# S5 block scan as a one-level tree, and GpSimd's share of the stage on VectorE

## The chip, the cores and the metric

The kernel runs on one core of a Trainium2 chip. The metric is the device time of one execution in microseconds (us), lower is better. Five engines take part: TensorE (PE, with its weight loads PEld), VectorE (DVE), ScalarE (ACT), GpSimd (POOL) and SyncE (SP, which here only issues transfers). Each engine runs its own instructions in order. DVE, ACT, POOL, SP and PE wait for one another by semaphores.

## The reference, cut to what matters

One encoder block over 1024 positions of width 1024. After a norm, one projection gives the columns z, xBC and dt of a Mamba-2 head group, and u of an S5 head group. Only the S5 scan is touched by the change. It has 64 channel groups, each with 64 complex states, and runs in both directions:

```python
bu_re = einsum("blgh,gph->blgp", ug, bb_re)        # and bu_im
_, _, h_re, h_im = lax.associative_scan(_complex_linear_combine, (a_re, a_im, bu_re, bu_im), axis=1)
y = einsum("blgp,ghp->blgh", h_re, c_re) - einsum("blgp,ghp->blgh", h_im, c_im)
```

That is the recurrence h[t] = a h[t-1] + bu[t] with a constant complex a for each state. After it follow a gated linear unit, the output projection and a feed-forward part, none of which the change touches.

## The kernel before, in words

**The scan.** The 1024 positions are cut into 128 blocks of 8. A matmul per block yields the block's own sum of states; a recurrence over the 128 blocks, with a to the eighth power (rcA real, rcB imaginary), turns the sums into the states at the block ends. They lie in one tile `SH` of 128 partitions by [direction 2, block 128, component 2, group pair 32], f32. A step of the recurrence (`rec_step`, L621 to 631) takes both directions at once: four VectorE operations of 128 elements a partition, two products (L628, L629) and two sums (L630, L631). There are 127 steps.

**The batch stage** (about 96 to 216 us of the profile). `s_batch(b)`, b = 0 to 7, makes the block sums of 8 groups: VectorE builds powers times B (L542 to 544, 896 elements each), PE transposes them (L550), ACT copies (L551), PE multiplies with u (L558), ACT copies the result into `SH` (L561), one element every 256 bytes. The tile `bp` between VectorE and PE has one buffer. Between the batches stand projection blocks on PE (`u_block`, `xbc_block`). This part is ordered by the planner from priorities and its own cost model; `sA` and `sB` are priorities for weight splits, `sb` for batches.

**The block stage** (about 216 to 434 us), under `tc.manual_schedule()`: the order on each engine is the order of the program text. 18 blocks n = 0 to 17: nine of xBC, one of dt, eight of z. An xBC or z block is 48 matmuls of 512 columns: three for each of 8 row chunks and two halves, because each weight is split in two f32r parts, `whi` (an ACT cast, L267) and `wlo` (raw minus whi, L268, one operation of 1024 elements). `wlo` is POOL's for xBC and z (`pl` = XZ), VectorE's elsewhere. `ensure` issues the split of block n+1 at the head of block n. ACT copies the two halves out of PSUM (L595 for xBC, L604 for z). After a block's matmuls the text has `run_steps(8)`, then one piece of the convolution `convs()`: on even n up to 10 a scaling on ACT (L719) and four VectorE operations (L724); on odd n the ACT silu of that result (L735), its store by SP (L737) and the load of the next channel block. For n = 11 to 14 it also has `c_dir`, 3 operations of 512 elements for each of two directions (L673 to 675), on POOL for these four batches (`pcd`), and one block later the small products `k_mm` (L692) on PE. The steps end with n = 15.

**The y stage** (about 442 to 545 us), also in text order: `restack` copies `SH` into `AH` (L770, eight copies for each of 16 batches, seven of them ACT's), `y_mm` multiplies with a table W0 (L780) and with AH (L781, L782), ACT applies gelu (L789). Then follow the gated unit, the Mamba-2 units, the output projection and the feed-forward part, up to 1695 us.

Of the kernel before, what the change touches and what calls it, by code (L numbers as in the profile page):

```python
# [9 lines left out]
F32 = mybir.dt.float32  # L10
# [5 lines left out]
ADD, SUB, MUL = ALU.add, ALU.subtract, ALU.mult  # L16


def _ap(t, off, dims):

    return bass.AP(tensor=t.tensor, offset=t.offset + off, ap=[list(t.ap[0])] + [list(d) for d in dims])
# [3 lines left out]
KN = {'s0': -800,  # L25
 'sA': 8,
 'sB': 50,
 'sG': -8,
 'sF': 20,
 'rec': 0,  # L30
 'cb': 8,
 'kb': -100,
 'w0': 0,
# [39 lines left out]
 'mq': 's',  # L73
 'pd': ['ef00', 'm00', 'xw1', 'yz0'],
 'yo': 0,
 'gst': 0,
 'g4': 800,
 'g6': -8,
# [1 line left out]
 'h6': 800,  # L80
 'fs': 0,
 'mc': 0,
 'pl': 'XZ',
 'pcd': [0, 1, 2, 3, 4, 5, 6, 7],
 'cd': [0, 1, 2, 3],
 'cB': [9, 11, 0, 1, 2, 3],
 'xq': 0,
# [1 line left out]
 'pc': [],  # L89
 'pk': [0, 1, 3, 4],  # L90
 'KC': 7,
 'r1': 8,
 'r2': 0,
 'r3': 0,
 'gs': 'asssssss',
 'gt': 'sasasasa',
# [36 lines left out]
def hymba_block(ctx, tc, P, out, dbg=None, upto=99):  # L133
    nc = tc.nc

    @contextmanager
    def hpri(n):
        off = KN[n]
        if off:
            p = tc.cur_priority  # L140
            tc.cur_priority = p - off
        yield
        if off:
            tc.cur_priority = tc.cur_priority + off

    def pri(n):
        def deco(f):
            def g(*a, **k):
                with hpri(n):
                    return f(*a, **k)  # L150
            return g
        return deco

    act, dve, pool, pe, sp = nc.scalar, nc.vector, nc.gpsimd, nc.tensor, nc.sync
# [10 lines left out]
    def newstack():  # L165
        e = ExitStack()
        stacks.append(e)
        return e
# [29 lines left out]
    def pacc():  # L198
        return psA.tile([128, 512], F32, tag="acc", name="acc")

    def ptmp():
        return psB.tile([128, 512], F32, tag="tmp", name="ptmp")
# [91 lines left out]
    rcA = rep.tile([128, 2, 2, 32], F32, name="rcA")  # L294
    rcB = rep.tile([128, 2, 2, 32], F32, name="rcB")
# [221 lines left out]
    @pri("lu")  # L517
    def load_u(b):
        U = sa.tile([128, 8, 128], F32, tag="U", name="U")
        sp.dma_start(U, u_d[8 * b:8 * b + 8].rearrange("g s h k -> (s h) g k"))  # L520
        return U

    def pw4(t, d, n0, nn, g0, ng):

        v = t[:, n0 - 1:n0 - 1 + nn, 64 * d + g0:64 * d + g0 + ng].rearrange("p n g -> p g n")
        return v.unsqueeze(3).to_broadcast([128, ng, nn, 16])

    def spread(t, nn):
        return t.unsqueeze(2).to_broadcast([t.shape[0], t.shape[1], nn, 16])

    @pri("sb")
    def s_batch(b, U):
        g0 = 8 * b
        yt = sa.tile([128, 2, 2, 8, 16], F32, tag="yt", name="yt")
        for y in range(2):
            sp.dma_start(yt[:, y].rearrange("p d g h -> p d (g h)"), y12_d[y][:, :, 16 * g0:16 * g0 + 128])
        bp = sa.tile([128, 2, 8, 8, 16], F32, tag="bp", name="bp")
        tm = sa.tile([128, 8, 7, 16], F32, tag="tmb", name="tmb")
        act.copy(_ap(bp, 0, [[1024 + 16 * 7, 2], [128, 8], [1, 16]]), yt[:, 0])
        for d in range(2):  # L540
            dst = _ap(bp, 16 if d == 0 else 1024 + 96, [[128, 8], [16 if d == 0 else -16, 7], [1, 16]])
            dve.tensor_tensor(dst, spread(yt[:, 0, d], 7), pw4(arR, d, 1, 7, g0, 8), op=MUL)  # L542
            dve.tensor_tensor(tm, spread(yt[:, 1, d], 7), pw4(aiR, d, 1, 7, g0, 8), op=MUL)
            dve.tensor_tensor(dst, dst, tm, op=ADD)
        for hb in range(2):
            bm = sa.tile([128, 2, 4, 128], F32, tag="bm", name="bm")
            for d in range(2):
                t = ptmp()
                for g in range(4):
                    pe.transpose(t[:, 128 * g:128 * g + 128], bp[:, d, 4 * hb + g].rearrange("p s h -> p (s h)"), ident)  # L550
                act.copy(bm[:, d].rearrange("p g c -> p (g c)"), t)  # L551
            for q in range(2):
                t = ptmp()
                for d in range(2):
                    for comp in range(2):
                        for j in range(2):
                            g = 2 * q + j
                            pe.matmul(t[64 * j:64 * j + 64, 256 * d + 128 * comp:256 * d + 128 * comp + 128],  # L558
                                      bm[:, d, g, 64 * comp:64 * comp + 64], U[:, 4 * hb + g, :], start=True, stop=True)
                pq = (g0 + 4 * hb + 2 * q) // 2  # L560
                act.copy(SH[:, :, :, :, pq].rearrange("p d k c -> p d c k"),  # L561
                         t.rearrange("p (d c k) -> p d c k", d=2, c=2))
# [6 lines left out]
    def u_half(b, hf):  # L569
        ps = pacc()  # L570
        gemm(b, hTh[hf], hTl[hf], HF[0], ps)
        u_evac(b, hf, ps)
# [10 lines left out]
    def u_block(b):  # L583
        ensure(b + 1)
        for hf in range(2):
            u_half(b, hf)

    def xbc_block(i):
        b = XORD[i]
        ensure(XBC0 + i + 1)  # L590
        xp = io.tile([128, 1024], F32, tag="io", name="xp")
        for hf in range(2):
            ps = pacc()
            gemm(XBC0 + i, hTh[hf], hTl[hf], HF[0], ps)
            act.copy(xp[:, HF[hf]], ps)  # L595
        aq.dma_start(xbc_d[128 * b:128 * b + 128, :], xp)
# [23 lines left out]
    @pri("rec")  # L620
    def rec_step(j):  # L621
        def at(k, swap=False):

            return _ap(SH, 64 * k + (32 if swap else 0),
                       [[8192 + 64 * (127 - 2 * k), 2], [-32 if swap else 32, 2], [1, 32]])
        m = rt.tile([128, 2, 2, 32], F32, tag="rm", name="rm", bufs=2)
        n = rt.tile([128, 2, 2, 32], F32, tag="rn", name="rn", bufs=2)
        dve.tensor_tensor(n, rcB, at(j - 1, True), op=MUL)  # L628
        dve.tensor_tensor(m, rcA, at(j - 1), op=MUL)  # L629
        dve.tensor_tensor(n, n, at(j), op=ADD)  # L630
        dve.tensor_tensor(at(j), m, n, op=ADD)  # L631

    steps = iter(range(1, 128))

    def run_steps(n):
        for _ in range(n):
            j = next(steps, None)
            if j is not None:
                rec_step(j)
# [39 lines left out]
    @pri("kb")  # L679
    def k_batch(b):  # L680
        k_mm(b)
        k_out(b)
# [49 lines left out]
    @pri("cs")  # L732
    def conv_silu(ct, xp, a, one=False, store=True):
        if one:
            act.activation(a, a, AF.Silu, scale=2.0)  # L735
            if store:
              sp.dma_start(xs_d[128 * ct:128 * ct + 128, :], a)  # L737
            return
        act.activation(xp, a, AF.Tanh)
        dve.scalar_tensor_tensor(a, xp, 1.0, a, op0=ADD, op1=MUL)  # L740
        if store:
            sp.dma_start(xs_d[128 * ct:128 * ct + 128, :], a)
# [500 lines left out]
    SH = shp.tile([128, 2, 128, 2, 32], F32, name="SH")  # L1243
    sst = newstack()
    sa = sst.enter_context(tc.tile_pool(name="sa", bufs=1, side="right"))
    for b in range(3, 8):
        s_batch(b - 3, load_u(b - 3))
        u_block(b)
    cv = None
    for b in range(5, 8):  # L1250
        s_batch(b, load_u(b))
        xbc_block(b - 5)
        if cv:
            conv_silu(*cv, one=True)
        if b > 5:
            cv = conv_taps(XORD[b - 6], sa)
    conv_silu(*cv, one=True)
    sst.close()
    ckst = newstack()
    ck = ckst.enter_context(tc.tile_pool(name="ck", bufs=1, side="right"))  # L1260
    rst = newstack()
    xt_load(0)
    rt = rst.enter_context(tc.tile_pool(name="rt", bufs=1, side="right"))
# [34 lines left out]

    cvs = convs()
    KC = KN["KC"]  # L1300
    with tc.manual_schedule():
        next(cvs)
        for n, blk in enumerate(blocks):
            blk()
            run_steps(KN["r1"])
            next(cvs, None)
            run_steps(KN["r2"])
            b = n - NB + KC
            if 0 <= b < 4:
                c_open(b)  # L1310
                c_dir(b, 0)
                run_steps(KN["r3"])
                c_dir(b, 1)
            if 0 < b < 4:
                k_batch(b - 1)
            if 0 <= b + 1 < 5 and n < NB - 1:
                xt_load(b + 1)
        run_steps(127)
        if KC == 4:
            xt_load(4)  # L1320
        next(cvs, None)
# [292 lines left out]
    def at(t, fn, *a):  # L1614
        tl.append((t, len(tl), fn, a))
# [104 lines left out]
    for l in range(8):  # L1720
        b = MX["step"] * l
# [11 lines left out]
        for q in range(2):  # L1733
            at(b + MX["ev"] + 0.6 * q, turn_evac, l, q)
            if l < 4 or q:
                n = "12"[q] + "12"[l // 4]
# [29 lines left out]
    for i in range(4, 14):  # L1766
        t = 2.56 * (i - 4)
# [13 lines left out]
    for i in range(14, len(prods)):  # L1781
        p, n, m = prods[i]
# [186 lines left out]
```

## Time and profile before

| | us |
|---|---|
| median of 3 runs | 1693.84 (1693.69 to 1709.21) |
| the profiled execution, its own time | 1697.36 |
| its span, first to last instruction | 1695.7 |
| PE busy | 1557.0 (92%) |
| VectorE busy | 1252.1 (74%) |
| ScalarE busy | 728.0 (43%) |
| GpSimd busy | 537.6 (32%) |

The busy shares are means over all stages. In the rows further down, a line names the code line, engine, operation, tile written and tiles read; "x" a count; a bracket at the end of a timeline row the idle time of the engine before it and what ended that. A row of busy time by stage has the stretch, its length, the busy us (and instructions) of PE, PEld, DVE, ACT and POOL, the granted clock as a share of full speed, the DMA share and GB/s.

### The profile page before, as it was taken

The numbers are of one execution on the slowest core, as the hardware profiler recorded it, in microseconds if no ns is written. First come the engines' busy times: TensorE is split into PE (matmuls) and PEld (weight loads), VectorE is DVE, ScalarE is ACT, GpSimd is POOL, SyncE is SP. The second block draws the span as 40 slices with busy tenths as digits, with TensorE's granted clock in tenths as the row PEclk, the third lists the DMA queues.
The fourth block names the chain that finished last, engine by engine and source line by source line (L and its number), as shares of the span: only waits on it lengthen the run. The fifth ranks groups of instructions, "written<-read, shape, count | busy, mean of one in ns | idle before, by whom it ended". The sixth has DMA issues, their size and how long they took to land.

```text
span 1695.7 us, 22363 instructions
## 1 busy us (share of the span) xinstructions
PE 1557.0 (92%) x7980; PEld 1270.2 (75%) x7980; DVE 1252.1 (74%) x2022; ACT 728.0 (43%) x1238; POOL 537.6 (32%) x499
## 2 busy tenths in 40 slices
PE   7998999889787879999998997999999999999897
PEld 6777788668675666778787775788888888787686
DVE  7445589999862567887576578788888788669777
ACT  6354632122598445444343277322222232344352
POOL 2111121157121020112111041555555555239512
PEclk9999999989799889999999998999999999999999
DMA  6543343243687748777668892333322221592234
GB/s 182 155 134 107 115 153 124 94 128 98 151 210 191 210 129 273 242 245 244 194 217 267 282 297 72 104 119 122 106 100 94 100 100 56 203 341 71 94 111 175
DMA packets 250003, 271.61 MB, mean 160 GB/s; under 512 B 29387, under 2 KB 190659, under 8 KB 249891
## 3 DMA queue, kind: packets, MB, share of 16 engines
q1 hardware_dynamic: 224515, 215.96, 41.2%
q0 software_dynamic: 12896, 33.83, 6.3%
q10 hardware_dynamic: 12480, 20.39, 3.4%
q8 instruction: 63, 1.03, 0.3%
q14 instruction: 49, 0.40, 0.1%
HBM read 185.23 MB, written 84.84 MB: 159 GB/s over the span
## 4 chain that ended last, share of the span: by engine, by line
PE 39%; DVE 10%; DMA 8%; issue 4%; ACT 3%; POOL 3%; SPq 0%; DVEq 0%; POOLq 0%; ACTq 0%
PE acc L1550 13%; PE ptmp L1550 10%; PE acc L1137 4%; PE ptmp L1856 4%; PE acc L1856 3%; DVE dop L1838 2%; DMA m<-m_d 2%; PE acc L277 1%; PE ptmp L956 1%; POOL wd L1823 1%; DMA m_d<-m 1%; DMA cl_d<-ghl 1%; DVE cacc L724 1%; PE ptmp L1022 1%; DMA graw<-g_d 1%
## 5 line engine op out<-in xcount | busy, mean ns | idle before, releaser
L277 PE MATMUL acc<-hTh,whi 128*128 128x512 f32 (+1 forms) x456 | 179.9, 395 | 8.5 <-ACT whi L267 8.0
L1137 PE MATMUL acc<-ohi,cat 128*128 128x512 f32 x512 | 175.7, 409 | 8.6 <-DMA cat<-ch_d 5.5
L277 PE MATMUL acc<-hTh,wlo 128*128 128x512 f32 (+1 forms) x456 | 179.1, 393 | 2.2 <-POOL wlo L268 2.1
L277 PE MATMUL acc<-hTl,whi 128*128 128x512 f32 (+1 forms) x456 | 179.4, 394 | 0.5 <-DVE hTl L337 0.5
L1533 DVE TENSOR_TENSOR wop<-rawp,wop 128x512 fp32r<-128x512 f32 x120 | 137.7, 1148 | 17.9 <-ACT wop L1532 16.7
L1550 PE MATMUL ptmp<-T,wop 128*128 128x512 f32 x528 | 127.9, 399 | 4.1 <-ACT T L1706 3.7
L1550 PE MATMUL acc<-T,wop 128*128 128x512 f32 x528 | 125.7, 393 | 1.6 <-DVE T L1709 1.5
L1856 PE MATMUL ptmp<-dop 128*128 128x512 f32 x528 | 122.2, 393 | 2.9 <-DVE dop L1838 2.9
L1550 PE MATMUL acc<-B,wop 128*128 128x512 f32 x528 | 124.6, 392 | 0.0
L1137 PEld LDWEIGHTS acc<-ohi,cat 128*128 128x128 f32 x512 | 99.3, 195 | 33.2 <-DVE s L1673 4.4
L1550 PEld LDWEIGHTS ptmp<-T,wop 128*128 128x128 f32 x528 | 101.2, 192 | 27.2 <-ACT T L1706 3.9
L268 POOL TENSOR_TENSOR wlo<-raw,whi 128x1024 fp32r<-128x1024 f32 x20 | 50.3, 2514 | 222.4 <-ACT whi L267 222.4
L1856 PEld LDWEIGHTS ptmp<-dop 128*128 128x128 f32 x528 | 100.2, 190 | 24.2 <-DVE dop L1838 3.2
L1550 PEld LDWEIGHTS acc<-T,wop 128*128 128x128 f32 x528 | 98.8, 188 | 24.9 <-DVE T L1709 3.3
L1550 PEld LDWEIGHTS acc<-B,wop 128*128 128x128 f32 x528 | 99.1, 188 | 21.7 <-DVE B L1709 0.2
L277 PEld LDWEIGHTS acc<-hTh,whi 128*128 128x128 f32 x456 | 87.1, 191 | 27.0 <-ACT whi L267 8.4
L1565 ACT ACTIVATE cg<-cg 128x512 f32<-128x512 f32 x44 | 27.8, 633 | 183.0 <-DVE cg L1563 182.9
L1838 DVE TENSOR_TENSOR dop<-da,dop 128x512 fp32r<-128x512 f32 x77 | 76.9, 999 | 36.7 <-ACT dop L1837 36.7
L1571 POOL TENSOR_TENSOR cg<-cg 128x512 f32<-128x512 f32 x44 | 61.8, 1405 | 130.5 <-DVE cg L1566 129.8
L277 PEld LDWEIGHTS acc<-hTh,wlo 128*128 128x128 f32 x456 | 87.1, 191 | 21.5 <-POOL wlo L268 4.1
L1532 ACT CAST wop<-rawp 128x512 fp32r<-128x512 f32 x120 | 70.2, 615 | 76.7 <-POOL rawp L1507 51.2
L1137 PE MATMUL acc<-olo,cat 128*128 128x512 f32 x256 | 103.1, 403 | 0.0
(362 smaller groups left out, 3566.1 us busy)
## 6 DMA issues: line engine op xcount, KB each, us to landing
ff_d<-cg POOLq DMA_DIRECT2D x77, 256.0 KB, 2.3
da<-ff_d SPq DMA_DIRECT2D x35, 512.0 KB
raw<-in_w_in_dram SPq DMA_DIRECT2D x28, 512.0 KB
cat<-ch_d SPq DMA_DIRECT2D x48, 256.0 KB
cat<-cl_d SPq DMA_DIRECT2D x48, 256.0 KB
wd<-in_w_down_dram SPq DMA_DIRECT2D x44, 256.0 KB
rawp<-in_w_gate_dram SPq DMA_DIRECT2D x10, 1024.0 KB
rawp<-in_w_up_dram SPq DMA_DIRECT2D x10, 1024.0 KB
```

The lines of the kernel that those rows point to most:

```text
L268: (pool if ("0" if j < 2 else "A" if j < XBC0 else "X" if j < Z0 else "Z" if j < GL0 else "G" if j < FF0 else "F") in KN['pl'] else dve).t ...
L277: pe.matmul(ps, a[:, k, :], b[:, k, sl], start=(k == 0 and n == 0), stop=(k == 7 and n == 2))
L724: (pool if ct in KN['pc'] and k in KN['pk'] else dve).scalar_tensor_tensor(a[:, d], xp[:, r], w[k], a[:, d], op0=MUL, op1=ADD)
L956: pe.matmul(t[:, 256 * s + 128 * d:256 * s + 128 * d + 128], Bt[:, c, g, :], Xw[:, d, c].rearrange("p h e -> p (h e)"), start=True, stop=True)
L1137: pe.matmul(ps, c[:, a, k % 4, :], b[:, k % 2, :], start=(k == 0 and n == 0), stop=(k == n_ - 1 and n == 2))
L1532: act.copy(t[:, 0], src)
L1533: dve.tensor_tensor(t[:, 1], src, t.bitcast(F32)[:, 0], op=SUB)
L1550: pe.matmul(ps, a[:, ai, k, :], b[:, bi, k, :], start=(k == 0 and q == 0), stop=(k == 3 and q == 2))
L1565: act.activation(cg[:, 0], cg[:, 0], AF.Silu)
L1571: pool.tensor_tensor(dst, a, b, op=op)
L1838: dve.tensor_tensor(t[:, k, 1], src, t.bitcast(F32)[:, k, 0], op=SUB)
L1856: pe.matmul(ps, t[:, 0, a, 128 * j:128 * j + 128], t[:, 1, b, :], start=(q == 0 and n == 0), stop=(q == NP - 1 and n == 2))
```

## The change

The scan becomes a tree of one level. (1) `pair_up(b)`, one for each of the 8 group batches and placed one batch behind `s_batch`, adds a times the first block's sum of each pair to the second's: 2 directions times 4 VectorE operations of 512 elements (64 pairs, 2 components, 4 group pairs). (2) `pair_powers` squares the power once: four operations of 128 elements. (3) `rec_step` runs over the 64 pair ends, 63 steps of the same four operations; 6 steps follow a block instead of 8, so that they end with n = 10. (4) `pair_down(d, c)` computes the 63 inner states of a direction from the pair ends: 8 calls of 4 operations of 1008 elements, one after each of the blocks 11 to 14, two after 15 and 16. (5) `pl` and `pcd` are emptied: 20 weight splits and 24 `c_dir` operations go from GpSimd to VectorE. The tile `up2` lies in the batch stage's pool `sa`, the tile `dn` shares the one buffer `cacc` with the convolution.

```diff
- 'pl': 'XZ',
- 'pcd': [0, 1, 2, 3, 4, 5, 6, 7],
+ 'pl': '',
+ 'pcd': [],
- 'r1': 8,
- 'r2': 0,
+ 'r1': 6,
...
-            return _ap(SH, 64 * k + (32 if swap else 0),
-                       [[8192 + 64 * (127 - 2 * k), 2], [-32 if swap else 32, 2], [1, 32]])
+            return _ap(SH, 64 * (2 * k + 1) + (32 if swap else 0),
+                       [[8192 + 64 * (125 - 4 * k), 2], [-32 if swap else 32, 2], [1, 32]])
...
-        dve.tensor_tensor(n, rcB, at(j - 1, True), op=MUL)
-        dve.tensor_tensor(m, rcA, at(j - 1), op=MUL)
+        dve.tensor_tensor(n, rcs[1], at(j - 1, True), op=MUL)
+        dve.tensor_tensor(m, rcs[0], at(j - 1), op=MUL)
...
-    steps = iter(range(1, 128))
+    steps = iter(range(1, 64))
+    rcs = []
+    def pair_powers():
...
+        dve.tensor_tensor(t, rcB, rcB, op=MUL)
+        dve.tensor_tensor(a2, rcA, rcA, op=MUL)
+        dve.tensor_tensor(a2, a2, t, op=SUB)
+        dve.scalar_tensor_tensor(b2, rcA, 2.0, rcB, op0=MUL, op1=MUL)
+    def advance(d, cur, prev, nk, q0, nq, t):
+        def at(k, swap=False):
+            return _ap(SH, 8192 * d + 64 * k + q0 + (32 if swap else 0), [[128, nk], [-32 if swap else 32, 2], [1, nq]])
+        for f, swap in ((rcA, False), (rcB, True)):
+            dve.tensor_tensor(t, f[:, d, :, q0:q0 + nq].unsqueeze(1).to_broadcast([128, nk, 2, nq]), at(prev, swap), op=MUL)
+            dve.tensor_tensor(at(cur), at(cur), t, op=ADD)
+    @pri("up")
+    def pair_up(b):
+        for d in range(2):
+            t = sa.tile([128, 64, 2, 4], F32, tag="up2", name="up2")
+            advance(d, 1 - d, d, 64, 4 * b, 4, t)
+    def pair_down(d, c):
+        t = ck.tile([128, 63, 2, 8], F32, tag="cacc", name="dn")
+        advance(d, 2 - d, 1 + d, 63, 8 * c, 8, t)
...
         s_batch(b - 3, load_u(b - 3))
+        if b > 3:
+            pair_up(b - 4)
         u_block(b)
...
         s_batch(b, load_u(b))
+        pair_up(b - 1)
         xbc_block(b - 5)
...
     conv_silu(*cv, one=True)
+    pair_up(7)
     sst.close()
...
         next(cvs)
+        pair_powers()
         for n, blk in enumerate(blocks):
             blk()
             run_steps(KN["r1"])
             next(cvs, None)
-            run_steps(KN["r2"])
+            if n == 10:
+                run_steps(64)
+            if n > 10:
+                for _ in range(1 if n < 15 else 2):
+                    if downs:
+                        pair_down(*downs.pop(0))
...
-        run_steps(127)
```

## Rows read from the trace of the kernel before

**Rows 1.** Busy time of each engine by stage: batch, block and y stage.
```profile
96.00:216.00 120.00, 113.06 (x898) 90.31 (x897) 69.00 (x68) 67.63 (x94) 15.70 (x13) 0.97 0.39 110
216.00:434.00 218.00, 203.19 (x934) 163.59 (x934) 204.51 (x492) 52.03 (x72) 76.91 (x59) 0.97 0.40 124
442.00:545.00 103.00, 79.32 (x718) 71.91 (x718) 53.27 (x88) 97.10 (x171) 21.83 (x40) 0.89 0.78 193
```

**Rows 2.** What PE waited for in the block stage.
```profile
PE acc L277 <- ACT whi L267: 8.0, 1, 8.0
PE ptmp L692 <- issue: 4.6, 1, 4.6
PE acc L277 <- POOL wlo L268: 2.1, 2, 1.3
```

**Rows 3.** ACT in order of time: copies of batch and block results, waits.
```profile
208.78 1.09 ACT L561 COPY SH<-ptmp 128x512 f32<-128x512 f32 x1
...
218.39 0.41 ACT L1267 CAST dtw<-dtr 128x256 fp32r<-128x256 f32 x1 [0.74 <-DMA xs_d<-cacc]
...
238.05 0.59 ACT L595 COPY xp<-acc 128x512 f32<-128x512 f32 x1 [4.85 <-PE acc L277]
...
248.93 0.59 ACT L595 COPY xp<-acc 128x512 f32<-128x512 f32 x1 [4.85 <-PE acc L277]
...
339.60 1.06 ACT L735 ACTIVATE cacc<-cacc 128x1024 f32<-128x1024 f32 x1 [15.51 <-DVE cacc L724]
...
441.51 4.57 ACT L770 COPY AH<-SH 64x254 f32<-64x254 f32 x7 [12.82 <-DVE SH L631]
```

**Rows 4.** PE in order of time, from the block stage into the y stage.
```profile
433.43 1.41 PE L692 MATMUL ptmp<-cp,yk 128*32 128x128 f32 x24
438.75 0.76 PE L780 MATMUL ptmp<-Uy,W 128*128 128x128 f32 x2 [3.92 <-issue]
```

**Rows 5.** VectorE in order of time: one undisturbed step, one disturbed product.
```profile
341.80 2.44 DVE L629 TENSOR_TENSOR rm<-rcA,SH 128x128 f32<-128x128 f32 x1
...
344.80 0.29 DVE L628 TENSOR_TENSOR rn<-rcB,SH 128x128 f32<-128x128 f32 x1
...
345.86 0.29 DVE L628 TENSOR_TENSOR rn<-rcB,SH 128x128 f32<-128x128 f32 x1
```

**Rows 6.** GpSimd in order of time, at the disturbed product.
```profile
341.67 2.42 POOL L268 TENSOR_TENSOR wlo<-raw,whi 128x1024 fp32r<-128x1024 f32 x1 [21.67 <-ACT whi L267]
```

**Rows 7.** VectorE's groups in the block stage, 216 to 443 us.
```profile
L629 DVE TENSOR_TENSOR rm<-rcA,SH 128x128 f32<-128x128 f32 x125 | 54.5, 436 | 0.0
L631 DVE TENSOR_TENSOR SH<-rm,rn 128x128 f32<-128x128 f32 x125 | 49.2, 393 | 4.3
...
L724 DVE SCALAR_TENSOR_TENSOR cacc<-xpad,vec,cacc 128x1022 f32<-128x1022 f32 x12 | 15.4, 1281 | 5.3 <-ACT cacc L719 5.1
```

**Rows 8.** GpSimd's groups in the block stage, 216 to 443 us.
```profile
L268 POOL TENSOR_TENSOR wlo<-raw,whi 128x1024 fp32r<-128x1024 f32 x16 | 39.2, 2450 | 138.0 <-ACT whi L267 137.9
L675 POOL TENSOR_TENSOR cp<-cp,tmc 128x512 f32<-128x512 f32 x8 | 11.4, 1429 | 0.6
...
L674 POOL TENSOR_TENSOR tmc<-xtc,aiR 128x512 f32<-128x512 f32 x8 | 9.1, 1142 | 0.0
```

**Rows 9.** VectorE over the whole span, shapes apart: split and c_dir there.
```profile
L268 DVE TENSOR_TENSOR wlo<-raw,whi 128x1024 fp32r<-128x1024 f32 x24 | 29.3, 1222 | 11.9 <-ACT whi L267 11.9
...
L673 DVE TENSOR_TENSOR cp<-xtc,arR 128x512 f32<-128x512 f32 x24 | 16.7, 695 | 15.5 <-DMA xtc<-x_d 15.2
```

**Rows 10.** VectorE's groups in the batch stage, 96 to 216 us.
```profile
L544 DVE TENSOR_TENSOR bp<-bp,tmb 128x896 f32<-128x896 f32 x16 | 21.7, 1355 | 0.2
...
L542 DVE TENSOR_TENSOR bp<-yt,arR 128x896 f32<-128x896 f32 x16 | 16.7, 1089 | 26.4 <-ACT bp L539 26.4
```

**Rows 11.** SP's queue in order of time: a convolution store.
```profile
215.58 0.33 SPq L737 DMA_DIRECT2D xs_d<-cacc  x1
```

More of the change, by code (lines that the diff above doesn't have):

```diff
@@ L75 @@
  'yo': 0,
+ 'up': 0,
  'gst': 0,
@@ L622, in at @@
         def at(k, swap=False):
-            return _ap(SH, 64 * k + (32 if swap else 0),
-                       [[8192 + 64 * (127 - 2 * k), 2], [-32 if swap else 32, 2], [1, 32]])
-        m = rt.tile([128, 2, 2, 32], F32, tag="rm", name="rm", bufs=2)
-        n = rt.tile([128, 2, 2, 32], F32, tag="rn", name="rn", bufs=2)
-        dve.tensor_tensor(n, rcB, at(j - 1, True), op=MUL)
-        dve.tensor_tensor(m, rcA, at(j - 1), op=MUL)
+            return _ap(SH, 64 * (2 * k + 1) + (32 if swap else 0),
+                       [[8192 + 64 * (125 - 4 * k), 2], [-32 if swap else 32, 2], [1, 32]])
+        m = rt.tile([128, 2, 2, 32], F32, tag="rm", name="rm")
+        n = rt.tile([128, 2, 2, 32], F32, tag="rn", name="rn")
+        dve.tensor_tensor(n, rcs[1], at(j - 1, True), op=MUL)
+        dve.tensor_tensor(m, rcs[0], at(j - 1), op=MUL)
         dve.tensor_tensor(n, n, at(j), op=ADD)
         dve.tensor_tensor(at(j), m, n, op=ADD)
-    steps = iter(range(1, 128))
+    steps = iter(range(1, 64))
+    rcs = []
+    def pair_powers():
+        t = rt.tile([128, 2, 2, 32], F32, tag="rm", name="rm")
+        a2 = rt.tile([128, 2, 2, 32], F32, name="rcA2")
+        b2 = rt.tile([128, 2, 2, 32], F32, name="rcB2")
+        dve.tensor_tensor(t, rcB, rcB, op=MUL)
+        dve.tensor_tensor(a2, rcA, rcA, op=MUL)
+        dve.tensor_tensor(a2, a2, t, op=SUB)
+        dve.scalar_tensor_tensor(b2, rcA, 2.0, rcB, op0=MUL, op1=MUL)
+        rcs.extend((a2, b2))
+    def advance(d, cur, prev, nk, q0, nq, t):
[12 more added lines that the diff above has]
+        advance(d, 2 - d, 1 + d, 63, 8 * c, 8, t)
     def run_steps(n):
@@ L1300, in hymba_block @@
     KC = KN["KC"]
+    downs = [(d, c) for c in range(4) for d in range(2)]
     with tc.manual_schedule():
         next(cvs)
+        pair_powers()
         for n, blk in enumerate(blocks):
```

## The prediction, made before the change was run

> **What bounds the kernel now.** I read busy time by stage first, then PE's waits, then the engine that the waits lead to. PE is busy 92% over all, so only a stage in which it stands still can give time. In the block stage [rows 1] PE lacks 14.8 us of 218, and VectorE is busy 204.5 of 218. PE's waits name others [rows 2]: 8.0 us for a weight cast on ACT, 4.6 at the small products, 2.1 for GpSimd's split. ACT is hardly loaded, so the cast was late for a reason: just ahead of it in ACT's order stands a silu that had waited 15.5 us for VectorE's convolution [rows 3]. The end of the stage is VectorE's too: the last matmul block ends at 433.4 [rows 4], but the restacking on ACT starts only at 441.5, released by the last step [rows 3]. Then ACT is busy 97 of 103 us [rows 1], so a y stage that begins earlier ends earlier by as much. In this stage VectorE sets the pace.
>
> Why is VectorE full? A step takes 1.06 us undisturbed, start to start [rows 5], and 127 make 135 us. But a product of 0.29 us lasted 2.44 while GpSimd ran a split of 2.42 us [rows 5, 6]. The steps' four groups (two of them stand in [rows 7]; the other two are like the second) hold about 54.5 + 3 x 49 = 201 us where 125 x 4 x 0.285 = 142 would do. So some 59 us of VectorE's busy time is waiting for GpSimd, whose splits and c_dir take 39.2 + 11.4 + 2 x 9.1 = 69 us there [rows 8]; the third c_dir group is like L674.
>
> **The change part by part.**
>
> *GpSimd's share.* 16 splits by 1.22 and 24 c_dir operations by 0.695 [rows 9] are 19.5 + 16.7 = 36 us on VectorE, against 59 us of waiting that goes: VectorE wins 23. GpSimd's order loses those operations; its small loads and stores come no later. A split is now behind VectorE's work of the block before; PE needs it about one block (10.88 us, [rows 3]) later.
>
> *Steps.* 64 fewer by 1.06 take 68 us off VectorE. The four operations of pair_powers cost 1.2.
>
> *Pair down.* 1008 elements: between 512 at 0.695 and 1024 at 1.222 [rows 9] a straight line gives 1.205, and with 0.03 between dependent operations 1.24. 8 x 4 x 1.24 = 40 us.
>
> *Pair up.* 512 elements at 0.695 + 0.03: 8 operations, 5.8 us for a batch, 46 us for eight. That is the batch stage's.
>
> The runs here are short: 8 adjacent elements below, 4 above; no row has VectorE on runs of 4. Low end: the 0.695 and 1.22 of [rows 9], since an operation of that size has not been seen cheaper. High end: ACT's copy into SH, with every element apart, took 1.09 against 0.59 for as many adjacent [rows 3], 1.85 times. I take the low end, because VectorE's own operations on runs of 16 [rows 10] say otherwise: 1.089 for 896 elements lies on the same line. [...]
>
> *The block stage, summed.* VectorE: steps 67, powers 1, down 40, splits 20, c_dir 17, convolution 24 x 1.28 = 31 [rows 7]: 176 us where it had 204. PE: its 203 busy us at a mean granted clock of 0.97 [rows 1] hide up to 203 x 0.03 = 6 us of low clock around its waits; I take 5. So PE could do the stage in 218 - 15 - 5 = 198 us. VectorE then has slack, and PE becomes the bound.
>
> *New waits.* (a) The last join starts when the last sums are in SH at 209.9 [rows 3] and after the four convolution operations that VectorE holds there, near 214.3; it ends near 220, the powers near 221.5. The block stage's tiles open only after it, where now they open when a store has landed, at 218.4 [rows 3]. The first split behind it is needed when block 0 ends, 238.05 - 10.88 = 227.2. Nothing is lost. (b) On even blocks the convolution waits for ACT's scaling after the block, so VectorE ends about 7 us behind PE; the next split comes 1.2 later, within 10.88. (c) The first pair_down shares its buffer with the last convolution: silu after block 11 (0.6 for the copy out, 1.06), then its store, which took from 215.58 to 218.39 [rows 3, 11], 2.8. So VectorE stands until 4.6 us after block 11, then needs 5.0 for pair_down and 6 x 0.695 = 4.2 for c_dir: 13.8. PE has finished block 12 at 10.88 and its k_mm stands for 2.9 us. Queued behind it is block 13. After that VectorE needs about 10.3 us a block and PE 10.88 plus k_mm: no more waits. VectorE is done some 6 us before the last block.
>
> PE's stage: 15 + 5 - 3 = 17 us sooner. *Handover.* PE's first product of the y stage waits for the table W0 until 5.3 us after the blocks [rows 4] and still will; but the restacking need no longer trail the blocks by 441.5 - 433.4 = 8.1, and can follow the last copy out at 0.6. ACT paces the stage, so 7.5 us more. What is late next there is W0, then ACT itself.
>
> *The batch stage.* VectorE idles 120 - 69 = 51 us [rows 1]. Seven joins (41) and four splits (5), less the waits for GpSimd in L544 (16 x (1.355 - 1.089) = 4, [rows 10]), make 42. The cover is VectorE's pause while PE and ACT work on a batch; a pause that is shorter than a join delays the next batch's products. I charge 3 us. Without cover the price is 46.
>
> Sum: -17 - 7.5 + 3 = -21.5. Against the profiled execution's 1697.36 that is 1675.9; it stood 3.5 above the median, and from 1693.84 I come to **1672 us**.
>
> **The rivals.**
>
> *Rival 1: joins stand in front of the next batch.* They come one batch behind, read SH while ACT writes its other columns, and their place in VectorE's order is the planner's. If half of each join (2.9 us) delays the next batch seven times, 20 us of the gain go: 1692. For it: little VectorE time is left over (42 of 51), and its products feed PE through one buffer. Against it: what delays L542 now is ACT [rows 10], a pause in which a join fits. Between this and the forecast every value from 1680 is possible.
>
> *Rival 2, the slower one: short runs cost as ACT's hopping does.* At 1.85 times, up is 85 us and down 73. The batch stage then needs 85 + 5 - 4 = 86 where 51 are idle: PE waits 35 us at the transposes. In the block stage VectorE has 209 us, more than PE's 198, so of the 24.5 only some 14 stay: 1693.84 + 35 - 14 = 1715. It decides once a join operation passes 51 / 56 = 0.9 us. For it: the ACT rows. Against it: VectorE's runs of 16 cost nothing extra.
>
> *Rival 3: the change frees VectorE but PE gains nothing,* because the cast waits for something else. Against it: the chain cast, silu, convolution is in the rows, and the 8.1 us at the end depend on no cast. Then only the 7.5 less the 3 would show: 1689. With rival 1 it lies within 1%.
>
> **How the numbers follow.** About 1% (17 us) is what a measurement of this kernel can tell from no change. Forecast 0.66: its own range is 1660 to 1682 (all of the batch stage's charge gone and 10 us more at the top, since low clock and waits may be undercounted; 10 us of lost charge below); 0.56 of it lies below 1677, 0.10 within 1%. Rivals 1 and 3 together 0.21, 1682 to 1694, of which 0.19 is within 1% and 0.02 faster. Rival 2 0.13: 0.12 slower, 0.01 within. Faster 0.58, same 0.30, slower 0.12. The range reaches over rivals 1 and 3 and leaves rival 2 and the edges out: 1660 to 1694.
>
> **What the profile after would show.** A step near 1.06 us everywhere in the block stage, no product of 2 us; 512-element joins near 0.7 and 1008-element ones near 1.2 (else rival 2); joins between L544 of one batch and L542 of the next, with PE's waits for L544 in the batch stage not above a few us (else rival 1); in the block stage no wait of 8 us for the cast, one of about 3 at k_mm; the blocks over near 416 to 419, the restacking right behind. I am wrong if PE's waits in the block stage stay at 15 us, if ACT still waits for VectorE at the restacking, or if the batch stage is over 10 us longer.

## The result, and the profile after

The changed kernel takes 1668.7 us (median of 4 runs, 1666.91 to 1674.15) against 1693.76 for the kernel before: 0.984 of it, 95% interval 0.981 to 0.987. That is 25 us by the medians, where the forecast was 22. The profiled execution took 1669.68 us, with a span of 1667.8.

Code lines from L634 on have moved by 32 to 43: the c_dir operations L673 to L675 are now L705 to L707, `k_mm` is L724 (was L692), the silu L767 (L735), the restacking L802 (L770), the W0 product L812 (L780), gelu L821 (L789). L652 is the product of a join, L653 its sum, both for `pair_up` and for `pair_down`.

Busy time by stage (as in [rows 1]); the last row is the y stage of this kernel, which begins 32 us sooner:

```profile
96.00:216.00 120.00, 116.56 (x928) 94.09 (x927) 105.95 (x125) 69.67 (x96) 4.70 (x9) 1.00 0.42 120
216.00:434.00 218.00, 207.83 (x1030) 170.36 (x1029) 177.31 (x372) 69.71 (x102) 13.49 (x27) 0.98 0.44 135
442.00:545.00 103.00, 77.62 (x606) 67.42 (x605) 47.41 (x81) 86.11 (x147) 20.23 (x34) 0.88 0.78 202
...
409.00:523.00 114.00, 88.17 (x773) 81.24 (x772) 54.32 (x86) 100.02 (x175) 24.84 (x47) 0.88 0.77 192
```

VectorE's work has moved from the block stage (204.5 to 177.3 us, and the stretch already holds the first 20 us of the y stage) into the batch stage (69.0 to 106.0), and PE is busier in both. PE's waits from 100 to 440 us, to be read beside [rows 2]:

```profile
PE ptmp L812 <- issue: 4.3, 1, 4.3
PE ptmp L558 <- ACT bm L551: 3.3, 6, 1.0
PE ptmp L724 <- issue: 3.3, 1, 3.3
PE ptmp L903 <- ACT AH L802: 2.6, 1, 2.6
```

The waits for a split or a cast are gone. What is left in the block stage is one at `k_mm`. VectorE's groups from 96 to 440 us, shapes apart:

```profile
L268 DVE TENSOR_TENSOR wlo<-raw,whi 128x1024 fp32r<-128x1024 f32 x22 | 26.8, 1219 | 1.7 <-ACT whi L267 1.7
L653 DVE TENSOR_TENSOR SH<-SH,up 128x512 f32<-128x512 f32 x32 | 22.0, 688 | 0.6
L653 DVE TENSOR_TENSOR SH<-SH,dn 128x1008 f32<-128x1008 f32 x16 | 19.3, 1208 | 0.6
L631 DVE TENSOR_TENSOR SH<-rm,rn 128x128 f32<-128x128 f32 x63 | 18.4, 292 | 2.2
...
L542 DVE TENSOR_TENSOR bp<-yt,arR 128x896 f32<-128x896 f32 x16 | 16.9, 1085 | 4.9 <-ACT bp L539 4.9
...
L652 DVE TENSOR_TENSOR dn<-rcA,SH 128x1008 f32<-128x1008 f32 x8 | 9.6, 1204 | 7.4 <-DMA xs_d<-cacc 7.4
```

The joins cost 688 and 1208 ns, the steps 292 where [rows 7] has 393 to 436, and before L542 VectorE now idles 4.9 us instead of 26.4 [rows 10]: that pause holds the joins. Four marks of each profile, in us, taken from the rows of ACT and PE in order of time, show where the time came from:

| | last copy of block 0 starts | last block matmul starts | last gelu is over | span |
|---|---|---|---|---|
| before | 227.17 | 433.11 | 546.25 | 1695.7 |
| after | 222.12 | 413.90 | 522.79 | 1667.8 |
| won since the mark before | 5.1 | 14.2 | 4.3 | 4.5 |
| after, run again beside later experiments | 227.62 | 418.27 | 528.83 | 1676.8 |
| won since the mark before | -0.5 | 15.3 | 2.6 | 1.5 |

The executions of before and after stood 3.5 and 1.0 us above their medians, the one run again 7.2. The 14 to 15 us at the blocks come in both executions of the changed kernel; the 5.1 ahead of them do not, so one execution tells the other stages to a few us only. What is won behind the last gelu belongs to the executions shown more than to the change: from there to the end it is 1149.5 us in the profile of before, 1145.0 in that of after, 1148.0 when it was run again, and 1143.9 to 1149.3 in the other ten experiments, one of them the kernel before with one edit ahead of this point (1146.9) and one with another (1146.4).

### The profile page after: what moved, and what is told of

It reads as the page before. It is cut to its first block, busy times and chain, and to the rows that moved or that the text cites. A ratio compares the mean times of both kernels' runs of the same rounds, so it can differ in the third digit from the quotient of the medians.

```text
span 1667.8 us, 22199 instructions
## 1 busy us (share of the span) xinstructions
PE 1546.0 (93%) x7980; PEld 1263.7 (76%) x7980; DVE 1241.3 (74%) x1910; ACT 730.4 (44%) x1238; POOL 461.4 (28%) x455
## 4 chain that ended last, share of the span: by engine, by line
PE 40%; DVE 10%; DMA 8%; issue 4%; ACT 4%; POOL 3%; SPq 0%; DVEq 0%; POOLq 0%; ACTq 0%
PE acc L1592 13%; PE ptmp L1592 10%; PE ptmp L1898 4%; PE acc L1169 3%; PE acc L1898 3%; DVE dop L1880 2%; PE acc L277 2%; DMA m<-m_d 2%; PE ptmp L988 1%; POOL wd L1865 1%; PE ptmp L1054 1%; DMA m_d<-m 1%; DMA oraw<-in_w_out_dram 1%; DVE cacc L756 1%; PE ptmp L1040 1%
## 5 line engine op out<-in xcount | busy, mean ns | idle before, releaser
L1898 PE MATMUL acc<-dop 128*128 128x512 f32 x396 | 95.6, 398 | 7.4 <-DVE dop L1880 4.7
L277 PEld LDWEIGHTS acc<-hTl,whi 128*128 128x128 f32 x456 | 86.7, 190 | 18.4 <-DVE hTl L337 1.0
```

What stands on the lines that cost most here:

```text
L277: pe.matmul(ps, a[:, k, :], b[:, k, sl], start=(k == 0 and n == 0), stop=(k == 7 and n == 2))
L1898: pe.matmul(ps, t[:, 0, a, 128 * j:128 * j + 128], t[:, 1, b, :], start=(q == 0 and n == 0), stop=(q == NP - 1 and n == 2))
```

## The experiments

Theory: before, VectorE set the pace of the block stage through two independent costs, the long chain of steps and its waiting for GpSimd. Each half of the change removes one, and the joins cost nothing because VectorE's pause in the batch stage takes them. Rivals: one half does it all; or the halves only work together; or the joins' price is small wherever they stand.

**One half each.** First GpSimd's share alone, in the kernel before:

```diff
- 'pl': 'XZ',
- 'pcd': [0, 1, 2, 3, 4, 5, 6, 7],
+ 'pl': '',
+ 'pcd': [],
```

> The kernel before with GpSimd's splits and c_dir on VectorE, and no tree: 127 steps as before. Theory (VectorE's sum decides, both parts are needed): VectorE has 135 + 36 + 31 = 202 us in the block stage, still more than PE's 198, and the splits now stand behind 8.5 us of steps a block, so the last block ends no sooner than about 430 (433.4 before); the steps end earlier, near 420, so the 8 us at the restacking go, and the batch stage loses its waits for GpSimd. 8 to 13 us of the 25 are won: 1681 to 1686. Rival A (the waiting for GpSimd was all there was): 1669, as the whole change. Rival B (the tree is all): 1693. In the trace a step lasts 1.06 us everywhere.

Then the tree alone: the changed kernel with both switches set back to `'XZ'` and `[0, 1, 2, 3, 4, 5, 6, 7]`.

> The changed kernel with the 20 splits and 24 c_dir operations back on GpSimd: the tree alone. Theory: VectorE has 67 + 1 + 40 + 31 = 139 us in the block stage plus 40 to 55 of waiting for GpSimd, 180 to 195, just under PE's 198, so most of the gain stays: 1670 to 1678, with some 2-us waits of PE for VectorE in the batch stage. Rival A (the waiting for GpSimd was all there was): 1690 or more, since the waiting stays. Rival B (the tree is all): 1668.

Measured: GpSimd's share alone 1686.09, 0.991 of before on the same chip [0.989, 0.994], 13 us by the medians and 15 by the ratio, at the upper edge of the 8 to 13 expected or above it; the tree alone 1680.18, 0.989 [0.984, 0.994], 18.5 us, as expected; both, run again unchanged beside later experiments, 0.982 [0.977, 0.987]. So neither half does it all. As a whole the two nearly add, but the marks of the profiles, as above, show that they do not add stage by stage. Won since the mark before, in us:

| | last copy of block 0 | last block matmul | last gelu | end of the span |
|---|---|---|---|---|
| GpSimd's share alone | 5.7 | 3.3 | -1.5 | 2.6 |
| the tree alone | 4.6 | 5.4 | 4.0 | 3.2 |
| both | 5.1 | 14.2 | 4.3 | 4.5 |
| both, run again | -0.5 | 15.3 | 2.6 | 1.5 |

At the blocks the halves win 3.3 and 5.4 us and both together 14 to 15: there the second rival, that the halves work only together, holds in part. Ahead of the blocks each half wins as much as both. That the totals nearly add is luck. One row of PE's waits with GpSimd's share alone:

```profile
PE acc L277 <- DVE wlo L268: 8.7, 4, 2.9
```

Its busy time in the block stage (columns as in [rows 1]):

```profile
216.00:434.00 218.00, 198.79 (x932) 160.26 (x931) 190.53 (x571) 60.97 (x87) 8.27 (x20) 0.98 0.42 126
```

Without GpSimd beside it a step's products take 283 ns (L629, in the profile's groups), the last block matmul starts at 424.09 instead of 433.11 (no sooner than 430 was expected), yet PE waits for VectorE's splits: 127 steps still pace the stage. VectorE is still busy 190.5 us there, where the changed kernel has 177.3. In the tree alone PE waits for GpSimd instead:

```profile
PE acc L277 <- POOL wlo L268: 9.4, 3, 5.9
```

VectorE and GpSimd lengthen each other's operations. Groups of POOL, then of DVE, in this kernel, from 100 and 96 to 443 us:

```profile
L268 POOL TENSOR_TENSOR wlo<-raw,whi 128x1024 fp32r<-128x1024 f32 x20 | 57.3, 2867 | 178.2 <-ACT whi L267 178.1
L707 POOL TENSOR_TENSOR cp<-cp,tmc 128x512 f32<-128x512 f32 x8 | 16.2, 2030 | 0.6
L706 POOL TENSOR_TENSOR tmc<-xtc,aiR 128x512 f32<-128x512 f32 x8 | 15.6, 1953 | 0.0
L705 POOL TENSOR_TENSOR cp<-xtc,arR 128x512 f32<-128x512 f32 x8 | 14.5, 1808 | 0.2 <-DMA xtc<-x_d 0.2
...
L653 DVE TENSOR_TENSOR SH<-SH,dn 128x1008 f32<-128x1008 f32 x16 | 29.1, 1816 | 0.6
```

The wide joins take 1816 ns where they took 1208, and c_dir on GpSimd 1808 to 2030 where it took 1142 to 1429 beside short steps [rows 8]. Its last block matmul starts at 423.11.

**c_dir back on GpSimd.** Is the whole of GpSimd's share needed? In the changed kernel:

```diff
- 'pcd': [],
+ 'pcd': [0, 1, 2, 3, 4, 5, 6, 7],
```

> The changed kernel with only the 24 c_dir operations back on GpSimd, the splits staying on VectorE. They would stand beside pair_down from block 11 on. Theory (the two engines block each other operation by operation, as in the run with the tree alone, where c_dir took 2.07 and pair_down 1.99 us): a block's c_dir takes 6 x 2.07 = 12.4 on GpSimd, as long as PE's block with k_mm; pair_down takes 8 us a block; so PE waits little, VectorE is done later: 0 to 5 us more than the changed kernel. Rival (c_dir out of VectorE's way helps k_mm, the wait for the store no longer delays it): 2 to 5 us less.

Its control is the changed kernel once more:

> The changed kernel as it is, as the yardstick for the three beside it: 0.984 of the kernel before.

Measured: 1677.23, 0.985 [0.981, 0.989], against 1671.30, 0.982 [0.977, 0.987], for the control on the same chip. The intervals overlap; a gain, the rival, is unlikely, and 6 us of loss (0 to 5 were expected) stand as an indication only. In the profiles the stretch from the last copy of block 0 to the last block matmul is 194.9 us, against 191.8 and 190.7 in the two of the changed kernel. VectorE is relieved of 17 us of c_dir and its splits still come late: PE waits 6.3 us for `wlo` (L268, one wait).

**The joins without their cover.** All eight `pair_up` calls at the head of the block stage:

```diff
-            t = sa.tile([128, 64, 2, 4], F32, tag="up2", name="up2")
+            t = ck.tile([128, 64, 2, 4], F32, tag="cacc", name="up2")
...
-        if b > 3:
-            pair_up(b - 4)
...
-        pair_up(b - 1)
...
-    pair_up(7)
...
+        for b in range(8):
+            pair_up(b)
         pair_powers()
```

> The changed kernel with all eight pair_up calls taken out of the batch stage and put at the head of the block stage, ahead of pair_powers, where nothing covers them. Theory (the joins are free only because VectorE has pauses in the batch stage): 46 us in a row from about 209; the split for the second block comes at about 257 where PE needs it at 222, so PE stands some 35 us, low clock behind it; the batch stage gives back at most 3: 1699 to 1706, the price of 46 less one block of lead. Rival (VectorE's slack in the block stage takes them up): under 1680.

Measured: 1714.9, 1.010 [1.006, 1.014]: slower than the kernel before, and 45 to 48 us, 2.6 to 2.8% of the time before, behind the changed one. The expectation (1699 to 1706) was too low: it had PE standing for some 35 us. VectorE in order of time (the bracket: its idle time before, and what ended it):

```profile
215.18 0.69 DVE L652 TENSOR_TENSOR up<-rcA,SH 128x512 f32<-128x512 f32 x1 [4.00 <-DMA xs_d<-cacc]
...
261.10 0.69 DVE L653 TENSOR_TENSOR SH<-SH,up 128x512 f32<-128x512 f32 x1
```

PE's wait for it:

```profile
PE acc L277 <- DVE wlo L268: 40.4, 1, 40.4
```

And that stretch, busy time and clock:

```profile
216.00:262.00 46.00, 7.49 (x34) 5.86 (x32) 43.89 (x66) 1.35 (x3) 2.54 (x4) 0.61 0.13 41
```

The 64 operations fill 46.6 us, as the prediction's price without cover (46) has it, and PE waits 40.4 us for the split behind them in VectorE's order; in these 46 us its mean granted clock is 0.61 of full speed. In the changed kernel the same operations cost nothing: two of them and their neighbours, VectorE in order of time:

```profile
115.27 1.09 DVE L544 TENSOR_TENSOR bp<-bp,tmb 128x896 f32<-128x896 f32 x1
116.27 0.69 DVE L652 TENSOR_TENSOR up<-rcA,SH 128x512 f32<-128x512 f32 x1
116.87 1.09 DVE L543 TENSOR_TENSOR tmb<-yt,aiR 128x896 f32<-128x896 f32 x1
117.88 0.69 DVE L653 TENSOR_TENSOR SH<-SH,up 128x512 f32<-128x512 f32 x1
118.48 1.09 DVE L544 TENSOR_TENSOR bp<-bp,tmb 128x896 f32<-128x896 f32 x1
```

They stand between the operations of a batch, one at a time, and PE has no wait for L544 in this stage (0.9 us when the changed kernel was run again).

**The wait at the first pair_down.** Its product shares the buffer `cacc` with the convolution. Give it another, `xpad`, which is free by then:

```diff
-        t = ck.tile([128, 63, 2, 8], F32, tag="cacc", name="dn")
+        t = ck.tile([128, 63, 2, 8], F32, tag="xpad", name="dn")
```

> The changed kernel, with the tile of pair_down in the buffer of the convolution's input (free once VectorE's last four convolution operations are through) in place of its output (free only when the store has landed). Theory: the wait of VectorE for that store goes (7.4 us in the trace after), with it PE's 3.3 us at k_mm after block 12 and the low clock behind it; the blocks after it come about 6 us sooner, and the y stage follows: 1663 to 1666. Rival: PE meets another late operand there or the y stage is tied to something that does not move with the blocks: 1668 to 1670.

In the changed kernel, VectorE and then PE at the point in question, in order of time:

```profile
343.57 1.21 DVE L652 TENSOR_TENSOR dn<-rcA,SH 128x1008 f32<-128x1008 f32 x1 [7.37 <-DMA xs_d<-cacc]
...
352.46 2.39 PE L724 MATMUL ptmp<-cp,yk 128*32 128x128 f32 x24 [3.26 <-issue]
```

With the other buffer:

```profile
335.67 1.22 DVE L268 TENSOR_TENSOR wlo<-raw,whi 128x1024 fp32r<-128x1024 f32 x1
336.80 1.20 DVE L652 TENSOR_TENSOR dn<-rcA,SH 128x1008 f32<-128x1008 f32 x1
```

The wait goes, and the last block matmul starts at 408.59, 5.3 us sooner. The whole shows little of it: 1667.45, 0.982 [0.979, 0.986], between what the theory and the rival expect. The last gelu is over 4.8 us sooner (518.01), and the rest of the span is 2.2 us longer; whether anything reaches the end the intervals don't tell.

**The y stage.** With the blocks over sooner, ACT's restacking copies should pace what follows. Part of them can be VectorE's, by two counts of the kernel (of 8 copies a batch, for batches 0 to 10 and 11 to 15; 1 and 0 in the kernel before and in the changed one). All with `xpad` as above, if not said otherwise:

```diff
- 'rsd': 1,
- 'rse': 0,
+ 'rsd': 3,
+ 'rse': 3,
```

With 2 and 2:

> The changed kernel with pair_down's tile in the input buffer, and VectorE taking 2 of the 8 copies of each restacking in all 16 batches (before: 1 of 8 in the first 11, none after). ACT loses 21 copies of 0.637 us, 13 us; VectorE, busy 35 of 80 us in the y stage, takes 21 more of 0.43. Theory (ACT paces the y stage, 72.6 of 80 us busy): the stage is 8 to 13 us shorter, the whole 1655 to 1660 where the changed kernel has 1669. Rival (the table loads and the operands of c_dir, for which VectorE waits 18 us there, pace it next): at most 4 us, 1663 to 1667.

With 3 and 3:

> The same with 3 of the 8 copies on VectorE. ACT loses 37 copies, 24 us. Theory (ACT paces): 1647 to 1655, less what PE (61 of 80 us busy at a clock of 0.87) or the transfers (share 0.79) now set. Rival: no more than with 2 copies, or worse, because VectorE's copies wait for PE to release AH and c_dir stands behind them: 1658 or more.

With 4 and 4:

> The changed kernel with the inner states' product in xpad and 4 of the 8 restacking copies of every batch on VectorE; ACT makes 64 of 128. Theory (PE paces the y stage once ACT has 80 or fewer): within 2 us of the version with 3, about 2.5% under the kernel before on the same chip. Rival 1 (ACT still paces): 3 to 5 us sooner than with 3. Rival 2 (VectorE's copies, which wait for the y products before they may overwrite AH, now trail): 3 us or more later.

With 3 and 3, but the product in `cacc` as in the changed kernel:

> The changed kernel with 3 of the 8 restacking copies of every batch on VectorE and the inner states' product in cacc as it is. Theory (the store wait at the first pair_down costs what the y stage gives back anyway): the same as with xpad within 3 us, that is 9 to 12 us under the changed kernel's median. Rival (with ACT off the path the 5 us at the first pair_down show in full): 5 us or more behind the version with xpad, 5 to 7 us under the changed kernel.

With 3 and 3 in the kernel before:

> The kernel before with 3 of the 8 restacking copies of every batch on VectorE instead of 1 or 0, so ACT makes 80 of the 128 copies and not 117. Theory (ACT paces the y stage in the kernel before as well, busy 97 of its 103 us): 37 copies of 0.637 us less on ACT are 23.6 us, of which PE can use about half before the table W0 and its own work hold it; the median falls by 8 to 12 us, as it did from the kernel with the inner states' product in xpad to the one with 3 copies on VectorE. The lever is then independent of the tree, and what the tree won must be counted without it. Rival (it pays only once the blocks end sooner and VectorE is free): at most 4 us, because VectorE still has c_dir and its last steps at the head of the stage.

| copies of 8 on VectorE | time, us | against before, same chip | last block matmul starts | last gelu over |
|---|---|---|---|---|
| 1, 0, `xpad` | 1667.45 | 0.982 [0.979, 0.986] | 408.59 | 518.01 |
| 2, 2, `xpad` | 1662.36 | 0.978 [0.974, 0.982] | 408.32 | 519.11 |
| 3, 3, `xpad` | 1657.13 | 0.974 [0.970, 0.978] | 411.04 | 509.98 |
| 4, 4, `xpad` | 1657.72 | 0.976 [0.973, 0.980] | 410.29 | 511.33 |
| 3, 3, `cacc` | 1660.87 | 0.978 [0.974, 0.981] | 413.71 | 511.79 |
| 3, 3, kernel before | 1686.00 | 0.992 [0.989, 0.995] | 435.29 | 538.63 |

Three copies are as good as four, and the stretch from the last block matmul to the end of the last gelu shrinks from 108.9 us (the changed kernel) to 98.9. The copies in groups of ACT and DVE, of the version with 3 and `xpad`, 380 to 560 and 410 to 560 us:

```profile
L802 ACT COPY AH<-SH 64x254 f32<-64x254 f32 x80 | 51.4, 642 | 1.5
...
L802 DVE COPY AH<-SH 64x254 f32<-64x254 f32 x45 | 18.8, 418 | 17.2 <-PE ptmp L814 16.4
```

It took 37 copies (117 to 80) of 0.64 us off ACT. The kernel before has the same lever: the stretch shrinks from 113.1 to 103.3 us there, and 13 to 15 us are won in all, where 8 to 12 were expected. So in both kernels, independently of the tree, 24 us less work on ACT shorten the stretch by 10: ACT's copies were part of what paced the y stage, but not all of it. With 2 and 2 and with 3 and 3 the medians lie between what theory and rival expect, and the profile with 2 and 2, an execution 6 us above its median, shows no shorter stretch (110.8 us); PE waits 7.6 us there for the table W0 and 6.5 for `cp` from ACT (L697). That the product in `cacc` costs 4 to 6 us with ACT out of the way (0.978 against 0.974) the intervals don't settle. The version with 3 and `xpad` has the lowest median here, 43 us under the kernel before; the one with 4 can't be told from it.

## Why the prediction was right

**What paced the block stage: right.** VectorE did, by both costs. The two halves, run alone, won 3.3 and 5.4 us in this stage, both together 14 to 15. With both, PE's waits for the cast and the split are gone; the one at the small products is 3.3 us where it was 4.6.

**The prices of VectorE's operations: right.** Up 688 ns (forecast 695), down 1208 (1205), splits 1219 (1222), a step's last sum 292. A step still starts 1.05 us after the one before, though the change also leaves its products `rm` and `rn` one buffer each where they had two. The sum of up and down by the rows was 86 us. Start to start, four ups run from 214.69 to 216.87, 0.73 each, and the downs of the first call from 343.57 to 347.30, 1.24 each: 64 x 0.73 + 32 x 1.24 = 86. Runs of four (688 ns) and of eight elements (1208 ns) cost nothing extra, and rival 2 fell.

**The block stage, forecast -17, measured -14.2 (-15.3 when run again).** The blocks are over at 414.3, where 416 to 419 was forecast, but they also began 5 us sooner. The wait at `k_mm` came as foreseen, 3.3 us against 2.9, from the store that the first pair_down waits for (7.4 of VectorE). What the term left out is the clock behind that wait, 0.81 of full speed from 350 to 368 us of the changed kernel:

```profile
350.00:368.00 18.00, 15.54 (x80) 12.41 (x81) 17.69 (x20) 2.54 (x5) 2.69 (x4) 0.81 0.37 112
```

With the wait gone (the run with `xpad`) the last block matmul starts 5.3 us sooner, so the wait cost about 5 and not 3. The rest of the term came out: without the wait it is 15 + 5 = 20 us, and in that run the stretch from the last copy of block 0 to the last block matmul is 185.8 us, where before it is 205.9.

**The handover, forecast -7.5, measured -4.3 (-2.6 when run again): the mis-sized term.** ACT in order of time, around the blocks' end:

```profile
403.44 0.60 ACT L604 ACTIVATE zt<-acc 128x512 f32<-128x512 f32 x1 [4.84 <-PE acc L277]
...
409.38 4.71 ACT L802 COPY AH<-SH 64x254 f32<-64x254 f32 x7
414.32 0.60 ACT L604 ACTIVATE zt<-acc 128x512 f32<-128x512 f32 x1 [0.24 <-PE acc L277]
...
416.29 4.55 ACT L802 COPY AH<-SH 64x254 f32<-64x254 f32 x7
```

What ACT waited for from 409 to 523 us:

```profile
ACT lg L730 <- issue: 6.5, 3, 4.6
ACT zt L604 <- PE acc L277: 5.1, 2, 4.8
ACT cp L697 <- DMA xtc<-x_d: 2.7, 1, 2.7
```

The restacking did follow at once; it even begins 4.5 us before the last block ends. But the step went on to say that ACT paces the stage, as if it would stay as full as before. It is busy 100.0 us of 114, with 14 us of waits, 4.6 of them in one wait at its copy of the small products (L730). PE's first W0 product starts 6 us behind the last block matmul and had waited 4.3 us: what the prediction named as late next. Of the 8 us of pause that went, so half or more did not reach the end of the stage. With GpSimd's share alone none did reach it: ACT's pause is gone there as well, but the stretch is 1.5 us longer than before, and in it PE waits 12.6 us at the small products for VectorE's c_dir (L675).

**The batch stage, forecast +3, measured -5.1 and, when run again, +0.5 at its end: wrong in sign, its size open.** From PE's first transposes (L550) to the last copy of block 0 it is 126.5 us before and 124.5 in the kernel before with 3 and 3 copies; it is 120.0 and 123.1 in the two profiles of the changed kernel. So the stage itself became 1.4 to 6.5 us shorter. The prediction counted the waits of L544 for GpSimd (4 us) as VectorE's alone. They were PE's. A stretch of this stage in the kernel before:

```profile
125.00:150.00 25.00, 22.67 (x198) 18.04 (x196) 13.39 (x12) 13.15 (x21) 4.58 (x4) 0.93 0.40 106
```

In it, GpSimd and VectorE in order of time:

```profile
125.96 3.05 POOL L268 TENSOR_TENSOR wlo<-raw,whi 128x1024 fp32r<-128x1024 f32 x1 [22.90 <-ACT whi L267]
126.81 3.16 DVE L544 TENSOR_TENSOR bp<-bp,tmb 128x896 f32<-128x896 f32 x1
```

And PE's wait for it in the whole stage:

```profile
PE ptmp L550 <- DVE bp L544: 4.8, 3, 2.1
```

The last L544 of a batch, which PE's transposes wait for, lasted 3.16 us beside a split, and PE's granted clock is 0.93 in this stretch. With GpSimd's share alone PE waits 0.4 us for L544, the clock stays at 1.00 and block 0 is copied out at 221.49. With the tree alone it is 1.4 us and 222.56, although GpSimd keeps its splits: they meet joins and one L543 there, and L544 takes 1083 ns where it took 1355 [rows 10].

**The joins' cover: right.** Rival 1 would have shown waits for L544; there are none, and 0.9 us when run again. The 3 us that were charged are not there, and without the cover the price is 45 us or more. **Rival 3** fell with PE's waits in the block stage: PE took what VectorE set free.

The errors (8 us more won in the batch stage, 3 less at the blocks, 3 less at the handover) nearly cancel: up to the last gelu 23.5 us were won where the sum had 21.5, and 17.4 when run again; the median came out 3 us under the forecast. The mechanism of the block stage was right; that the sum came so close is in part luck.

## What to carry to other kernels

When an engine that is not the busiest sets the pace of a stage, look for all the costs that make it full: here a long serial chain and a second engine beside it. Taken away alone, each freed 3 to 5 us of the stage, both together 14 to 15. Compare a sum with the trace stage by stage, since totals can agree when their terms don't. Wide work may be free in one stage and cost its whole length in another (the joins: 0 to 0.9 us of PE's waits under the batches, 45 us or more of the whole at the head of the blocks), so find the engine's pause first and put the work there. When the pause in front of an engine goes, forecast the waits inside its next stage as well, not only its busy time.

## What the runs showed of the hardware that was not expected

VectorE and GpSimd delay each other in both directions, operation by operation. In the tree alone, in order of time:

```profile
352.73 2.07 POOL L705 TENSOR_TENSOR cp<-xtc,arR 128x512 f32<-128x512 f32 x1
353.87 1.99 DVE L653 TENSOR_TENSOR SH<-SH,dn 128x1008 f32<-128x1008 f32 x1
354.75 2.07 POOL L706 TENSOR_TENSOR tmc<-xtc,aiR 128x512 f32<-128x512 f32 x1
355.89 1.99 DVE L652 TENSOR_TENSOR dn<-rcA,SH 128x1008 f32<-128x1008 f32 x1
```

Each lasts 2.0 to 2.1 us, and each ends about 1 us after the other engine's; alone the DVE operation takes 1.21 (343.57 in the changed kernel, above) and the POOL operation 1.11 (340.08 in the tree alone, where VectorE stands idle). In these rows the two engines take turns. They don't everywhere. In the batch stage of the same run, in order of time:

```profile
195.14 7.21 POOL L268 TENSOR_TENSOR wlo<-raw,whi 128x1024 fp32r<-128x1024 f32 x1 [22.08 <-ACT whi L267]
...
198.42 1.08 DVE L544 TENSOR_TENSOR bp<-bp,tmb 128x896 f32<-128x896 f32 x1
199.43 0.68 DVE L652 TENSOR_TENSOR up<-rcB,SH 128x512 f32<-128x512 f32 x1
200.14 2.75 DVE L653 TENSOR_TENSOR SH<-SH,up 128x512 f32<-128x512 f32 x1
```

The split lasts 7.21 us where the one at 120.71 takes 2.36, while six VectorE operations from 195.22 on keep their usual 0.68 to 1.08 us, each starting before the one ahead of it is over. The seventh needs the result of the sixth and starts 0.03 us behind its end; it lasts 2.75 us, and the split is over 2.2 us behind that gap. The split at 169.05 (4.01 us) shows the same, and the operations of pair_down above, which alternate with GpSimd's, each wait for the one before: a sum for its product, a product for the buffer that the sum still reads. As far as these rows go, GpSimd gets in where VectorE leaves such a gap, here 0.03 us; why, they do not show. The prediction had the delay in one direction only, since in its rows only VectorE's operations were seen to stretch (2.44 us for 0.29, [rows 5]).

The same restacking copy of 64 x 254 elements takes 0.42 us on VectorE and 0.64 on ACT.
